# Merge gates computed first, most of them in pairs with seven products, and kept in memory until the merge

## The chip, the cores and the metric

The kernel runs on one core of one Trainium2 chip. The metric is the device time of one execution in microseconds (us); three runs of the kernel before gave 1060.51, 1060.54 and 1064.07, a median of 1060.54. A core has a matmul engine (TensorE, "PE" in the profile, with its weight loads as "PEld"), three elementwise engines (VectorE "DVE", ScalarE "ACT", GpSimd "POOL"), a queue engine (SyncE, "SP") and DMA engines between main memory and the on-chip memory (SBUF). Matmuls write into a separate small memory, PSUM, here used as eight banks of 128 x 512 numbers.

## The reference, cut to what matters

One layer over 1024 prompt tokens and 32 sample tokens (1056 columns together), width 1024. `h` is the normalised input, `w_in` one combined projection of it:

```python
z = _rmsnorm(x, norm_w) @ w_in          # qa ka va ga | qb kb vb gb | uc gc | mg (3 * 1024 wide)
# A: sliding-window attention, B: dilated attention in three groups, C: pooling  ->  oa, ob, oc
ma, mb, mc = jnp.split(mg, 3, axis=-1)
pa = (oa * jax.nn.silu(ga)) @ w_proj_a
pb = (ob * jax.nn.silu(gb)) @ w_proj_b
pc = (oc * jax.nn.silu(gc)) @ w_proj_c
m = jax.nn.sigmoid(ma) * pa + jax.nn.sigmoid(mb) * pb + jax.nn.sigmoid(mc) * pc
y = _rmsnorm(x + m @ w_out, final_norm_w)
```

The three merge gates `ma`, `mb`, `mc` are 24 blocks of 128 output channels (8 for each branch); each is a product of a 1024 x 128 weight block with the 1024 x 1056 input. The kernel also returns updated key, value and pooling states for prompt and sample.

## The kernel before, in words

Everything is computed with channels on the 128 partitions and tokens along the free axis. All dense products are in full precision made of three products of numbers in a format named `fp32r`: a number is split into a high part (ScalarE copies it into the format) and a low part (VectorE subtracts the high part from it), and hi x hi, hi x lo and lo x hi are added in PSUM.

**Projection blocks.** `w_in` is laid out as 58 blocks of 128 columns. `w_load` (L133) fetches a block of 512 KB, `w_split` (L141) splits it with one ScalarE copy and one VectorE subtraction of 128 x 1024 numbers, and `proj_chunk` (L313, matmul at L319) makes 24 matmuls (8 slices of the input width, 3 parts) for a chunk of columns. The chunks `CH` are 384, 384 and 288 columns. `project` (L334) does a whole block: it splits the next block ahead, hands out two state copies (memory to memory, issued by GpSimd, L182) and calls the evacuation of each chunk.

**Order.** The kernel is written out by hand in one order (`manual_schedule`), and each engine's instructions stand in its queue as they are written. At the start, nine input tiles are normalised and transposed while the first three blocks (K, V and the first Q of A) are made in quarters of 256, 256, 256 and 288 columns. Then follow the other projections, with the attention as side work that is pumped between matmul groups (`tick`, `pump`); then the gates of the branches, with sample attention, pooling and the merging of B's groups beside them; then the merge; then the output projection (L1480, and L1518 for the last 256 tokens) with the final norm.

**The merge (loop at L1342).** For each of 8 output blocks j and each branch: the gate block is projected (72 matmuls), each chunk is taken through tanh (`merge_gate`, L1302, sigmoid by way of tanh), then `branch` (L1289, matmul at L1295) makes the branch product of the same chunk out of the gated branch outputs `ghi`, `glo` (12 matmuls a chunk for A, 6 for B and for C), and `merge_add` (L1307) multiplies both on VectorE (L1310) and adds onto block `m_t[j]` on GpSimd (L1312). The branch outputs of C are ready before the merge; those of B and A are made during it by `gate_plan`: `load_a` fetches an attention output and its scale (DMA on SyncE, product on GpSimd, L1244), `mult_a` (L1252) multiplies it with the gate, `high` and `low` (L1265, L1271) split it. The first output block therefore takes the branches in the order C, B, A, and the others A, B, C. The eight slices of `w_out` are loaded and split in the last output block (`out_load`, `out_split`), and `m_split` (L1333) splits the merged blocks for the output projection.

## Time and profile before

| | |
|---|---|
| median of three runs | 1060.54 us |
| profiled execution, its own time | 1061.22 us |
| its span (first to last instruction) | 1059.4 us |
| TensorE busy | 1032.9 us, 97% |
| VectorE, ScalarE, GpSimd busy | 434.5, 343.2, 219.2 us |
| mean granted TensorE clock | 0.996 |
| moved by DMA | 144.43 MB |

The profile is of one execution. "Busy" is the time in which an engine had an instruction in work. TensorE's matmuls are pipelined: each is drawn longer than the distance to the next, so the price of one is taken from the distance of their starts, as the chain of waits shows it for runs of matmuls. The chain is followed back from the last instruction to what released each step. In rows of the timeline, square brackets hold the engine's idle time before an instruction and what ended it.

### The profile page before, as it was taken

The numbers are of one execution on the slowest core, as the hardware profiler recorded it, in microseconds if no ns is written. First come the engines' busy times: TensorE is split into PE (matmuls) and PEld (weight loads), VectorE is DVE, ScalarE is ACT, GpSimd is POOL, SyncE is SP. The second block draws the span as 40 slices with busy tenths as digits, with TensorE's granted clock in tenths as the row PEclk, the third lists the DMA queues.
The fourth block names the chain that finished last, engine by engine and source line by source line (L and its number), as shares of the span: only waits on it lengthen the run. The fifth ranks groups of instructions, "written<-read, shape, count | busy, mean of one in ns | idle before, by whom it ended". The sixth has DMA issues, their size and how long they took to land.

```text
span 1059.4 us, 18173 instructions
## 1 busy us (share of the span) xinstructions
PE 1032.9 (97%) x7521; PEld 992.8 (94%) x7521; DVE 434.5 (41%) x923; ACT 343.2 (32%) x842; POOL 219.2 (21%) x321
## 2 busy tenths in 40 slices
...
GB/s 253 42 213 61 61 110 116 166 59 179 81 177 98 180 136 147 107 260 309 215 288 126 230 159 78 196 104 139 79 119 157 62 175 21 89 115 101 54 71 119
DMA packets 56302, 144.43 MB, mean 136 GB/s; under 512 B 13062, under 2 KB 31812, under 8 KB 54884
## 3 DMA queue, kind: packets, MB, share of 16 engines
...
## 4 chain that ended last, share of the span: by engine, by line
PE 85%; DMA 4%; DVE 4%; ACT 2%; POOL 2%; issue 1%; ACTq 0%; POOLq 0%; SPq 0%; DVEq 0%
PE ps_pj L319 56%; PE ps_pj L1480 6%; PE ps_s L1295 4%; PE ps_t L1295 4%; PE ps_s L518 3%; PE ps_o L560 3%; DMA w_in<-w_scr 3%; PE ps_t L538 2%; PE ps_pj L1518 1%; DMA kv<-in_st_b 1%; PE ps_s L1518 1%; ACT e L525 1%; DVE sq L294 1%; PE ps_o L881 1%; POOL o_in L1166 1%
## 5 line engine op out<-in xcount | busy, mean ns | idle before, releaser
L319 PE MATMUL ps_pj<-xh,w_hi 128*128 128x384 f32 (+2 forms) x1384 | 450.9, 332 | 1.1 <-ACT xh L307 0.5
L319 PE MATMUL ps_pj<-xl,w_hi 128*128 128x384 f32 (+2 forms) x1384 | 435.6, 321 | 1.3 <-DVE xl L308 1.3
L319 PE MATMUL ps_pj<-xh,w_lo 128*128 128x384 f32 (+2 forms) x1384 | 434.7, 321 | 0.0
L319 PEld LDWEIGHTS ps_pj<-xh,w_hi 128*128 128x128 f32 x1384 | 256.5, 188 | 10.1 <-issue 6.6
L319 PEld LDWEIGHTS ps_pj<-xl,w_hi 128*128 128x128 f32 x1384 | 256.6, 188 | 1.9 <-DVE xl L308 1.5
L319 PEld LDWEIGHTS ps_pj<-xh,w_lo 128*128 128x128 f32 x1384 | 256.1, 188 | 0.0
L150 DVE TENSOR_TENSOR w_lo<-w_raw,w_hi 128x1024 fp32r<-128x1024 f32 x55 | 70.0, 1273 | 201.6 <-ACT w_hi L149 201.4
L1304 ACT ACTIVATE mth<-ps_pj 128x384 f32<-128x384 f32 (+1 forms) x72 | 33.2, 463 | 249.5 <-PE ps_pj L319 246.7
L1312 POOL TENSOR_TENSOR m<-m,mth 128x384 f32<-128x384 f32 (+1 forms) x48 | 48.0, 1018 | 286.5 <-DVE mth L1310 286.3
L410 POOL TENSOR_SCALAR k<-k 64x384 fp32r<-64x384 f32 (+1 forms) x44 | 20.8, 474 | 287.9 <-ACT k L406 211.1
L525 ACT ACTIVATE e<-e,nm_b 128x256 f32<-128x256 f32 (+1 forms) x96 | 44.2, 461 | 62.9 <-DVE nm_b L522 62.5
L149 ACT ACTIVATE w_hi<-w_raw 128x1024 fp32r<-128x1024 f32 x55 | 58.0, 1054 | 1.0 <-PE ps_pj L319 1.0
L370 DVE SCALAR_TENSOR_TENSOR q<-ps_pj,q 64x384 fp32r<-64x384 f32 (+1 forms) x62 | 31.0, 500 | 54.1 <-ACT q L369 53.8
L518 PE MATMUL ps_s<-k,q 128*128 128x256 f32 x320 | 51.2, 283 | 0.0
L518 PEld LDWEIGHTS ps_s<-k,q 128*128 128x128 f32 x320 | 45.8, 188 | 0.3 <-issue 0.2
L369 ACT ACTIVATE q<-ps_pj 64x384 fp32r<-64x384 f32 (+1 forms) x62 | 27.1, 438 | 53.6 <-DVE q L370 29.4
L538 PE MATMUL ps_t<-ident,e 128*128 128x128 f32 x276 | 43.1, 273 | 1.1 <-DVE pt L545 0.6
L182 POOL DMA_DIRECT2D out_b_s<-in_st_b x84 | 42.2, 508 | 0.0
L525 ACT ACTIVATE e<-e,nm_a 128x256 f32<-128x256 f32 (+1 forms) x64 | 31.1, 487 | 30.1 <-DVE nm_a L522 30.1
L522 DVE CUSTOM_DVE_ANT_0 e<-ps_s,bias 128x256 f32<-128x256 f32 (+1 forms) x96 | 31.8, 371 | 15.4 <-PE ps_s L518 14.9
L538 PEld LDWEIGHTS ps_t<-ident,e 128*128 128x128 f32 x276 | 33.9, 141 | 3.8 <-ACT pt L543 1.2
L560 PE MATMUL ps_o<-pt,v 128*64 128x128 f32 x552 | 35.2, 277 | 2.1 <-DVE pt L545 2.1
...
## 6 DMA issues: line engine op xcount, KB each, us to landing
...
```

Of the source, the lines that this page charges most:

```text
L149: act.activation(out=hi, in_=raw, func=AF.Copy)
L150: eng.tensor_tensor(out=lo, in0=raw, in1=hi.bitcast(F32), op=ALU.subtract)
L182: pool.dma_start(out=dst, in_=src)
L319: pe.matmul(ps[:, :cn], lhsT=parts[p][0][:, k, :], rhs=parts[p][1][:, k, c0:c0 + cn], start=(step == 0), stop=(step == 23))
L518: pe.matmul(ps[:, 256 * hd:256 * hd + 256], lhsT=q, rhs=rhs, start=(i == 0), stop=(i == 1))
L525: act.activation(out=e[:, hd, :nk], in_=e[:, hd, :nk], func=AF.Exp, scale=-1.0, bias=nm, accum_out=z)
L538: pe.transpose(tp[:, o:o + 128], e[:, hd, 128 * k:128 * k + 128], ident)
L560: pe.matmul(ps[64 * hd:64 * hd + 64, c0:c0 + 128], lhsT=v[:, tl, 64 * hd:64 * hd + 64], rhs=pt[:, o:o + 128], start=(k == 0), stop=(k == n ...
L1295: pe.matmul(pp[:, :cn], lhsT=a[:, k, :], rhs=b[k][:, c0:c0 + cn], start=(step == 0), stop=(step == last))
L1304: act.activation(out=th[:, :cn], in_=ps[:, :cn], func=AF.Tanh, scale=0.5)
L1312: pool.tensor_tensor(out=dst, in0=dst, in1=th[:, :cn], op=ALU.add)
L1480: pe.matmul(ps[o][:, :cn], lhsT=wo[k][b][:, 128 * o:128 * o + 128], rhs=a[:, k, c0:c0 + cn], start=(k == 0 and si == 0), stop=(k == 7 and ...
```

## The change

The 24 merge gates are computed first, right behind the input's normalisation, and kept in memory (`g_scr`). Gates 0 to 2 take the place that K, V and Q had in the start, gate 3 follows as an ordinary block in quarters. The other 20 blocks are taken as 10 pairs. For a pair of blocks and two of four quarters of 264 columns, the four results (two blocks x two quarters) are made from seven products of half the width (512 of 1024) instead of eight, by sums of weight halves and sums of input halves (the scheme of Winograd's variant of Strassen's product). Ten pairs times two halves of the columns are 20 iterations. In each, GpSimd makes four sums of weights for the next iteration (`pair_sums`), ScalarE and VectorE split seven weight tiles of 128 x 512 (`pair_split`; the last subtraction goes to GpSimd), TensorE makes seven products of 12 matmuls with 264 columns, VectorE combines them (`plus`), ScalarE takes the tanh and SyncE stores it (`gate_of`). The input sums are made by `combos` on VectorE and GpSimd, and split by `combo_split`.

Afterwards K, V and Q follow as ordinary projections. In the merge no gates are projected: 24 steps of branch products alone, first C (8 blocks), then B (4 blocks), A (8 blocks) and B (4 blocks); the gates are loaded from memory by SyncE (`gate_load`) into the tiles that held the input. The branch weights `w_pr` are laid out in eight tiles by branch. The output weights are prepared over steps 12 to 23, two of their subtractions on GpSimd, and all merged blocks are split before the output projection.

```diff
+    def gate_evac(g):
+        def evac(c0, cn, ps):
+            th = st.tile([128, 288], F32, tag="g", name="gate_o", bufs=8)
+            act.activation(out=th[:, :cn], in_=ps[:, :cn], func=AF.Tanh, scale=0.5)
+            sp.dma_start(out=g_scr[g][:, c0:c0 + cn], in_=th[:, :cn])
+        return evac
...
+    def combos(c):
+        a, b = st.tile([128, 8, NQ], F32, tag="s", name="x_sum", bufs=6), None
+        t1, t3 = a[:, 0:4, :], a[:, 4:8, :]
+        b = st.tile([128, 8, NQ], F32, tag="s", name="x_sum", bufs=6)
+        t2, t4 = b[:, 0:4, :], b[:, 4:8, :]
+        (h11, l11), (h12, l12) = ([t.bitcast(F32) for t in xq(2 * c, h)] for h in range(2))
+        (h21, l21), (h22, l22) = ([t.bitcast(F32) for t in xq(2 * c + 1, h)] for h in range(2))
+        add, sub = ALU.add, ALU.subtract
+        todo = [(dve, t1, h21, h22, add), (pool, t3, h11, h21, sub), (dve, t1, t1, l21, add), (pool, t3, t3, l11, add),
+                (dve, t1, t1, l22, add), (pool, t3, t3, l21, sub), (dve, t2, t1, h11, sub), (dve, t2, t2, l11, sub),
+                (dve, t4, h12, t2, sub), (dve, t4, t4, l12, add)]
+        return {"sum": (t1, t2, t3, t4), "todo": todo}
+
+    def combo_step(c, eng=None):
+        if c["todo"]:
+            e, out, x, y, op = c["todo"].pop(0)
+            (eng or e).tensor_tensor(out=out, in0=x, in1=y, op=op)
+
+    def combo_split(c, i):
+        t = st.tile([128, 8, NQ], F32R, tag="s", name=f"x_s{i}", bufs=6)
+        src = c["sum"][i - 1]
+        act.activation(out=t[:, 0:4, :], in_=src, func=AF.Copy)
+        dve.tensor_tensor(out=t[:, 4:8, :], in0=src, in1=t[:, 0:4, :].bitcast(F32), op=ALU.subtract)
+        c[i] = (t[:, 0:4, :], t[:, 4:8, :])
...
+    def pair_of(it):
+        c, i = divmod(it, 10)
+        return c, 4 + 2 * i, 5 + 2 * i
+
+    def pair_load(it):
+        if it < 20:
+            _, g1, g2 = pair_of(it)
+            raw_p[it] = w_raw(g1), w_raw(g2, True)
...
+            if (c, w) == (2, 0):
+                cmb[0] = combos(0)
+            if c >= 2:
+                combo_step(cmb[0])
+                combo_step(cmb[0])
+            if (c, w) == (3, 0):
+                pair_load(0)
...
+    def pair_sums(it):
+        r1, r2 = raw_p[it]
+        t1, t2, t3, t4 = (st.tile([128, 4, 128], F32, tag="tt", name=f"w_t{i}", bufs=6) for i in range(4))
+        for out, x, y in ((t3, r2[:, 4:8], r2[:, 0:4]), (t1, r2[:, 0:4], r1[:, 0:4]), (t2, r2[:, 4:8], t1), (t4, r1[:, 4:8], t2)):
+            pool.tensor_tensor(out=out, in0=x, in1=y, op=ALU.subtract)
+        wt[it] = {"src": {"b11": r1[:, 0:4], "b21": r1[:, 4:8], "b22": r2[:, 4:8], "t1": t1, "t2": t2, "t3": t3, "t4": t4}}
+
+    def pair_split(it, name, eng=dve):
+        if it >= 20:
+            return
+        t = w_tile({"b11": "whi", "b22": "whi", "b21": "wlo", "t4": "wlo"}.get(name, "wc"))
+        src = wt[it]["src"][name]
+        act.activation(out=t[:, 0:4, :], in_=src, func=AF.Copy)
+        eng.tensor_tensor(out=t[:, 4:8, :], in0=src, in1=t[:, 0:4, :].bitcast(F32), op=ALU.subtract)
+        wt[it][name] = t
+
+    turn7 = [0]
+
+    def product(w, x):
+        ps = bank(("pj", "s", "t", "pj", "s", "t", "pj")[turn7[0] % 7])
+        turn7[0] += 1
+        n = 0
+        for k in range(4):
+            for wo_, xo in ((0, 0), (0, 1), (4, 0)):
+                pe.matmul(ps[:, :NQ], lhsT=w[:, wo_ + k, :], rhs=x[xo][:, k, :], start=(n == 0), stop=(n == 11))
+                n += 1
+        return ps[:, :NQ]
+
+    def part():
+        return st.tile([128, NQ], F32, tag="p", name="part", bufs=6)
+
+    def plus(ps, t, out=None):
+        out = part() if out is None else out
+        dve.tensor_tensor(out=out, in0=t, in1=ps, op=ALU.add)
+        return out
+
+    def gate_of(src, g, q):
+        act.activation(out=src, in_=src, func=AF.Tanh, scale=0.5)
+        sp.dma_start(out=g_scr[g][:, NQ * q:NQ * q + NQ], in_=src)
+
+    e3 = gate_evac(3)
+    pair_sums(0)
+    pair_load(1)
+    todo = [("b11", "b21"), ("t2", "t3"), ("t1",), ()]
+    for n, (c0, cn) in enumerate(quarters):
+        for ps in proj_chunk("g3", c0, cn):
+            pass
+        e3(c0, cn, ps)
+        for name in todo[n]:
+            pair_split(0, name)
+        combo_split(cmb[0], (2, 3, 1, 4)[n])
+    pair_split(0, "t4")
+    pair_split(0, "b22")
+    for it in range(20):
+        c, g1, g2 = pair_of(it)
+        q1, q2 = 2 * c, 2 * c + 1
+        w, x = wt[it], cmb[c]
+        nxt = it + 1
+        pair_load(it + 2)
+        if it >= 18:
+            w_load(it - 18)
+        state_copy(2)
+        if nxt < 20:
+            pair_sums(nxt)
+        ps = product(w["b11"], xq(q1, 0))
+        p1 = part()
+        act.activation(out=p1, in_=ps, func=AF.Copy)
+        ps = product(w["b21"], xq(q1, 1))
+        pair_split(nxt, "b11")
+        c11 = plus(ps, p1)
+        ps = product(w["t2"], x[2])
+        u2 = plus(ps, p1, p1)
+        gate_of(c11, g1, q1)
+        pair_split(nxt, "b21")
+        if it == 9:
+            combo_split(cmb[1], 2)
+        ps = product(w["t3"], x[3])
+        u3 = plus(ps, u2)
+        pair_split(nxt, "t2")
+        if it == 9:
+            combo_split(cmb[1], 3)
+        ps = product(w["t4"], xq(q2, 1))
+        gate_of(plus(ps, u3), g1, q2)
+        pair_split(nxt, "t3")
+        ps = product(w["t1"], x[1])
+        c22 = plus(ps, u3, u3)
+        u4 = plus(ps, u2, u2)
+        gate_of(c22, g2, q2)
+        if it == 9:
+            combo_split(cmb[1], 1)
+        pair_split(nxt, "t4")
+        ps = product(w["b22"], x[4])
+        pair_split(nxt, "t1")
+        gate_of(plus(ps, u4, u4), g2, q1)
+        pair_split(nxt, "b22", pool)
+        if it == 0:
+            cmb[1] = combos(1)
+        if it < 8:
+            combo_step(cmb[1])
+            if it in (6, 7):
+                combo_step(cmb[1])
+        if it == 9:
+            combo_split(cmb[1], 4)
+        if nxt == 20:
+            w_split(0)
...
+    make_bias(0)
+    project(0, evac_k(0), 0)
+    project(1, evac_v(0), 0)
+    for i in range(4):
+        if i:
+            make_bias(i)
         if i >= 2:
             flush_attention(i - 2)
-        project(2 + i, evac_q(i), 1.6, 2)
+        project(2 + i, evac_q(i), 1.6 if i else 0, 2)
...
+    xa, xb, xc, xd = (xtp.tile([128, 4, NT], F32, tag=tag, name="x_" + tag) for tag in ("xh0", "xl0", "xh1", "xl1"))
+    temp = [xa[:, i, :] for i in range(4)] + [xb[:, i, :] for i in range(3)]
+    gate_at = [xc[:, i, :] for i in range(4)] + [xd[:, i, :] for i in range(4)] + [xb[:, 3, :]]
+    steps = [(2, j) for j in range(8)] + [(1, j) for j in range(4)] + [(0, j) for j in range(8)] + [(1, j) for j in range(4, 8)]
+    place = list(range(8)) + [8, 0, 1, 2] + [(3 + i) % 8 for i in range(8)]
+    gate_t = {}
+
+    def gate_load(i):
+        if i < 20:
+            gate_t[i] = gate_at[place[i]]
+        else:
+            gate_t[i] = mp.tile([128, NT], F32, tag=f"g{i - 20}", name="gate") if i < 22 else slot_tile(i - 22, "gate")
+        br, j = steps[i]
+        sp.dma_start(out=gate_t[i], in_=g_scr[8 * br + j])
+
+    for i in range(3):
+        gate_load(i)
...
     def load_a(i, o_slot, w_slot):
         def run():
-            t = slot_tile(o_slot, "o_in")
+            t = temp[o_slot - 1]
             sp.dma_start(out=t[:, :L], in_=o_scr[i])
-            w = slot_tile(w_slot, "w_in")
+            w = temp[w_slot - 1]
...
+    def merge_add(i, c0, cn, pp):
+        br, j = steps[i]
+        th = gate_t[i][:, c0:c0 + cn]
         dst = m_t[j][:, c0:c0 + cn]
-        out = dst if bi == 0 else th[:, :cn]
-        dve.scalar_tensor_tensor(out=out, in0=th[:, :cn], scalar=1.0, in1=pp[:, :cn], op0=ALU.add, op1=ALU.mult)
-        if bi:
-            pool.tensor_tensor(out=dst, in0=dst, in1=th[:, :cn], op=ALU.add)
+        dve.scalar_tensor_tensor(out=dst if br == 2 else th, in0=th, scalar=1.0, in1=pp[:, :cn], op0=ALU.add, op1=ALU.mult)
+        if br != 2:
+            pool.tensor_tensor(out=dst, in0=dst, in1=th, op=ALU.add)
...
+    for i, (br, j) in enumerate(steps):
...
+        if i in (0, 4, 8, 12, 14, 16, 18):
+            n = 34 + (0, 4, 8, 12, 14, 16, 18).index(i)
+            w_split(n + 1)
+            w_load(n + 3)
+        for nxt in ((3, 4, 5, 6, 7, 8) if i == 0 else (i + 8,) if 1 <= i < 9 else (i + 7,) if 10 <= i < 13 else ()):
+            gate_load(nxt)
+        if br == 1 and j == 0:
+            while gates_done[0] < 2:
+                pump()
+        if br == 0 and j == 0:
+            while gates_done[0] < 6:
+                pump()
+        if i == 1:
+            zero = mp.tile([128, 128], F32, tag="g0", name="zero")
+            pool.memset(zero, 0.0)
+            for kv in range(2):
+                sp.dma_start(out=b3_p[kv, 0:1024, :].rearrange("(p a) (b c) -> p (a b) c", a=8, c=128),
+                             in_=zero.unsqueeze(1).to_broadcast([128, 16, 128]))
...
+        if i == 22:
+            out_split(5, r[5], gh, "h2", gl, "l4", pool)
+        if i == 23:
+            out_split(6, r[6], gh, "h3", gl, "l5", pool)
+        last = i == 23
+        for c0, cn in CH[::-1] if last else CH:
+            pp = branch(i, c0, cn)
+            tick(1.0)
+            merge_add(i, c0, cn, pp)
+            if last and c0:
+                m_split(7, c0, cn)
+                if c0 == 768:
+                    out_split(7, r[7], wr, "whi", wr, "wlo")
+        if i in (14, 15, 16, 17):
+            m_split(i - 14)
+        if i in (21, 22, 23):
+            m_split(i - 17)
+    m_split(7, 0, 384)
```

## Rows read from the trace of the kernel before

**Rows 1.** Page, busy us (share of the span) and instructions.
```profile
PE 1032.9 (97%) x7521; PEld 992.8 (94%) x7521; DVE 434.5 (41%) x923; ACT 343.2 (32%) x842; POOL 219.2 (21%) x321
```

**Rows 2.** Windows: stretch, length, busy us of each engine, granted clock, DMA share, GB/s.
```profile
494.00:520.00 26.00, 23.79 (x249) 21.97 (x251) 16.14 (x26) 8.36 (x17) 16.20 (x14) 1.00 0.84 273
624.00:650.00 26.00, 26.00 (x161) 26.00 (x160) 5.43 (x8) 3.89 (x6) 4.73 (x7) 1.00 0.38 125
```

**Rows 3.** Chain of waits in order of time: start us, us, what.
```profile
42.46 2.82 PE ps_pj L319 x24
...
595.22 11.62 PE ps_pj L319 x72
...
952.13 9.54 PE ps_pj L1480 x72
```

**Rows 4.** Timeline, TensorE: first matmuls of the stages' borders.
```profile
59.86 0.42 PE L319 MATMUL ps_pj<-xh,w_hi 128*128 128x384 f32 x1
...
580.55 0.34 PE L319 MATMUL ps_pj<-xh,w_hi 128*128 128x384 f32 x1
...
951.97 0.56 PE L1480 MATMUL ps_pj<-mh,wo_hi 128*128 128x288 f32 x3
```

**Rows 5.** Groups by line and shape, GpSimd: busy us, mean ns, idle before.
```profile
L182 POOL DMA_DIRECT2D out_b_s<-in_st_b x84 | 42.2, 508 | 0.0
L1312 POOL TENSOR_TENSOR m<-m,mth 128x384 f32<-128x384 f32 x32 | 34.7, 1090 | 277.4 <-DVE mth L1310 277.1
...
L1437 POOL TENSOR_TENSOR acc<-acc,sq_o 128x512 f32<-128x512 f32 x7 | 9.1, 1298 | 32.1 <-ACT sq_o L1436 32.1
```

**Rows 6.** Groups by line and shape, ScalarE.
```profile
L1304 ACT ACTIVATE mth<-ps_pj 128x288 f32<-128x288 f32 x24 | 9.9, 411 | 38.3 <-PE ps_pj L319 38.3
...
L1335 ACT ACTIVATE mh<-m 128x512 fp32r<-128x512 f32 x8 | 4.5, 615 | 0.0
```

**Rows 7.** VectorE: a PSUM addition (groups); a split of 512 (timeline).
```profile
L1430 DVE TENSOR_TENSOR x_res<-x_res,ps_pj 128x288 f32<-128x288 f32 x6 | 2.5, 448 | 3.4 <-PE ps_pj L1480 3.4
...
963.66 0.69 DVE L1336 TENSOR_TENSOR ml<-m,mh 128x512 fp32r<-128x512 f32 x1 [1.03 <-ACT mh L1335]
```

**Rows 8.** Timeline of ScalarE and VectorE, start of the kernel.
```profile
14.61 1.05 ACT L1010 ACTIVATE w_first<-w_raw 128x1024 fp32r<-128x1024 f32 x1
...
16.76 1.44 DVE L294 SCALAR_TENSOR_TENSOR sq<-x_nat,ss,nwb 128x512 f32<-128x512 f32 x2 [0.72 <-POOL ss L286]
18.13 1.21 DVE L1011 TENSOR_TENSOR w_first<-w_raw,w_first 128x1024 fp32r<-128x1024 f32 x1
```

**Rows 9.** Timeline of VectorE and GpSimd where both have work, merge.
```profile
593.51 2.40 POOL L1244 TENSOR_TENSOR o_in<-o_in,w_in 128x1024 f32<-128x1024 f32 x1 [2.23 <-DMA w_in<-rz_scr]
...
594.46 0.55 DVE L1310 SCALAR_TENSOR_TENSOR m<-mth,ps_s 128x384 f32<-128x384 f32 x1 [0.46 <-PE ps_s L1295]
...
605.06 2.40 POOL L1244 TENSOR_TENSOR o_in<-o_in,w_in 128x1024 f32<-128x1024 f32 x1 [0.65 <-DMA w_in<-rz_scr]
605.16 3.38 DVE L150 TENSOR_TENSOR w_lo<-w_raw,w_hi 128x1024 fp32r<-128x1024 f32 x1 [3.98 <-ACT w_hi L149]
```

**Rows 10.** Windows with much DMA: start of the kernel, start of the merge.
```profile
6.00:8.00 2.00, 1.63 (x12) 1.19 (x10) 1.41 (x2) 0.13 (x1) 0.34 (x1) 1.00 1.02 418
...
588.00:592.00 4.00, 4.00 (x30) 4.00 (x29) 1.35 (x1) 2.89 (x4) 2.40 (x1) 1.00 1.06 213
```

**Rows 11.** Timeline of SyncE's queue and GpSimd, start of the merge.
```profile
580.91 0.33 SPq L1239 DMA_DIRECT2D o_in<-o_scr  x1
...
588.88 2.40 POOL L1244 TENSOR_TENSOR o_in<-o_in,w_in 128x1024 f32<-128x1024 f32 x1 [44.15 <-DMA o_in<-o_scr]
```

More of the change, by code (lines that the diff above doesn't have):

```diff
@@ L316, in proj_chunk @@
         parts = ((hi, xh), (hi, xl), (lo, xh))
-        order = [(k, p) for p in range(3) for k in range(8)] if n < 3 else [(k, p) for k in range(8) for p in range(3)]
+        first = n in ("g0", "g1", "g2")
+        order = [(k, p) for p in range(3) for k in range(8)] if first else [(k, p) for k in range(8) for p in range(3)]
         for step, (k, p) in enumerate(order):
-            pe.matmul(ps[:, :cn], lhsT=parts[p][0][:, k, :], rhs=parts[p][1][:, k, c0:c0 + cn], start=(step == 0), stop=(step == 23))
-            if step % (8 if n < 3 else 6) == (7 if n < 3 else 5):
+            pe.matmul(ps[:, :cn], lhsT=parts[p][0][:, k, :], rhs=parts[p][1][k // 4][:, k % 4, c0:c0 + cn], start=(step == 0), stop=(step == 23))
+            if step % (8 if first else 6) == (7 if first else 5):
                 yield None
@@ L1040, in build @@
     x_turn(0)
-    w_first(0)
+    w_first("g0")
     x_turn(1)
-    w_first(1)
-    x_sq(2)
-    x_scale(2)
-    w_first(2)
-    x_sq(3)
-    x_scale(3)
-    first_e = (evac_k(0), evac_v(0), evac_q(0))
+    w_first("g1")
+    norm(2)
+    w_first("g2")
+    norm(3)
+    first_e = [gate_evac(g) for g in range(3)]
     c0, cn = quarters[0]
-    runs = [proj_chunk(w, c0, cn) for w in range(3)]
+    runs = [proj_chunk(f"g{w}", c0, cn) for w in range(3)]
     for w in range(3):
@@ L1076, in build @@
                 x_turn(8)
-            if (c, w) == (2, 1):
-                w_load(4)
             if (c, w) == (3, 0):
-                w_split(3)
+                splits["g3"] = w_tile("whi"), w_tile("wlo")
+                w_first("g3")
             first_e[w](c0, cn, ps)
@@ L1088, in build @@
+    close(st_cm)
+    gc1_cm, gc1 = open_pool("gc1")
+    at_cm, at0 = open_pool("attn")
+    at[0] = at0
+    up = [gc1.tile([128, 16 + NT], F32, tag=f"c{t}", name=f"up{t}") for t in range(2)]
     for t in range(2):
```

256 lines of the change are left out of this document (104 added, 152 removed).

## The prediction

> **What bounds the kernel now.** I read the busy shares first: TensorE 97%, the three elementwise engines 21 to 41% [rows 1]. By stretches, TensorE is busy for all 26 of 26 us in the merge at full granted clock, and even where it idles a little (23.79 of 26) the clock stays 1.00 [rows 2]. The chain of waits is TensorE nearly throughout, and it gives the price of a matmul: 24 of 256 columns in 2.82 us (118 ns each), 72 of 288 in 9.54 us (132.5 ns), a whole gate block of 72 (48 of 384 columns, 24 of 288) in 11.62 us [rows 3]. TensorE's order of time gives the borders: the three quartered blocks end at 59.9, the merge runs from 580.55 to 951.97, 371.4 us, of which 24 x 11.62 = 278.9 are gates and 92.5 branch products; nothing in it is a stall [rows 4]. So the kernel is TensorE-bound, and taking columns away pays as long as the other engines keep up.
>
> **The products.** A product of the paired stage is 12 matmuls of 264 columns. Between 118 and 132.5 ns that is 121.6 ns by interpolation, 1.46 us a product, 10.2 us for the seven of an iteration, 204.3 for 20 iterations. The 20 blocks cost 20 x 11.62 = 232.4 before. TensorE's own gain is 28.1 us. Gates 0 to 2 take the place of K, V and Q of pair 0 in the start at the same matmul counts; those three then cost what the three gates did; gate 3 in quarters costs 11.7 instead of 11.62.
>
> **The paired stage: a loop through the queues.** Busy time an iteration is small: VectorE six splits at 0.69 and seven additions at 0.43, 7.2 us [rows 7]; ScalarE seven copies at 0.615, four tanh and a copy at about 0.40 (288 columns took 0.41), 6.3 us [rows 6]; GpSimd five operations of 512 elements at 1.30 and two state-copy issues at 0.51, 7.5 us [rows 5]. All stand under 10.2, so by shares the stage would be TensorE's. But the engines take their work in the written order: a weight split that was ready when ScalarE finished at 15.66 stood behind a scale that waited for GpSimd, and ran at 18.13 [rows 8]. In the new loop that order closes a ring. GpSimd starts the sums for the next iteration only behind `pair_split(nxt,"b22",pool)` of the one before, and that split waits for ScalarE's copy of b22, which is queued behind the last tanh, which waits for VectorE's last addition, which is queued behind the splits of t1 and t4, t3 and t2; and t2 is what GpSimd's sums make. Once round:
> GpSimd: two state copies 1.02, sums t3, t1, t2 3.90;
> ScalarE copies t2 0.615; VectorE splits it 0.69 and adds product 5, 0.43; tanh 0.40;
> copy t3 0.615, split 0.69, add product 6, 0.43, tanh 0.40;
> copy t4 0.615, split t4 0.69, split t1 0.69 (its copy lies beside), add product 7, 0.43, tanh 0.40;
> copy b22 0.615; GpSimd splits it 1.30.
> GpSimd 6.22, ScalarE 3.66, VectorE 4.05: 13.9 us. An instruction's hand-on costs some 0.03 to 0.08, and back-to-back operations start about as much before the end of the one ahead; I set these against each other.
>
> To it comes the conflict of VectorE and GpSimd. A VectorE split that takes 1.21 to 1.23 alone took 3.38 beside a 2.40 us GpSimd operation that it met 0.1 after its start; an operation that reads PSUM took 0.55 beside one, its usual time [rows 9]. So splits and sums exclude each other, additions do not. Placed on the loop's clock, the sum t1 falls on the split of b21 (0.4 lost) and the split of t2 on the sum t4 (0.6 lost): 14.9 us an iteration. TensorE then idles 4.7 us in each. The Trainium skill (GPSIMD Engine Reference, section 3.1 Elementwise — side-by-side cycle accounting) puts a two-input operation at about 2.6 cycles an element at 1.2 GHz; as an estimate that is 1.1 us for 512 elements, and the loop would be 14.1. The row of 1.30 decides.
>
> The first three iterations run at 10.2 on weights and banks made ahead (seven PSUM banks hold one whole iteration): 30.6, then 17 x 14.9 = 253.3. The sums of x for the second half put three GpSimd operations of 1056 elements into the loop (2.40 for 1024 [rows 9]): about 8 with VectorE's. Iteration 9 puts four copies and splits of 1056 into it: 4.5 beyond what the idle hides. Stage: 297 us. Bounds: no conflict and no extras, 17 x 13.9 + 30.6 = 267; a conflict on each of the four splits in the ring, 16.3 an iteration and 20 of extras, 328. I take 297, since conflicts are seen wherever both engines have work.
>
> Data: 1 MB of weights, 0.54 of gates out and 1 of state copies are 2.6 MB an iteration; at the 213 GB/s that mixed traffic had [rows 10] 12.2 us, under 14.9. No cost, but no room either if the loop were as fast as TensorE.
>
> **Around it.** Start: fewer evacuations, but ten sums of 1056 elements between the turns of x; +1 (-2 to +4). Hand-over to K of pair 0: `w_split(0)` stands behind the last tanh, so TensorE waits for 0.2 + 0.43 + 0.40 + 1.05 (copy) + 1.21 (split) [rows 8] = 3.3 us (2 to 5). Attention, B, pooling and sample stages keep their work, 520.7 us; the state copies run out earlier, which nothing there waits for.
>
> **The merge.** Branch products alone, 92.5 us. In the merge before, GpSimd's first product of attention output waited for its data until 588.88 after an issue at 580.91 [rows 11], covered by gate products; this cover is gone. SyncE's queue now brings nine gates (4.9 MB) ahead of that data, then 4 MB of it, 2 MB of zeros and three gates more before A can start, with 1.5 MB of weights on ScalarE's queue: 14 MB. At 418 GB/s, the best seen, 33 us; at 300, 47; at 213, 66 [rows 10]. TensorE has 12 steps of 18/72 x 11.62 = 2.9, 34.9 us, before the A steps. After the last data come 2.4 + 1.3 + 1.1 + 1.3 = 6 us of preparation. I take +18 (3 to 30), by 300 GB/s: loads are purer than in the 213 stretch. While VectorE waits in `mult_a`, the C additions queue behind it.
>
> **Tail.** GpSimd adds three pieces a step at about 1.0 [rows 5], 3.0 against TensorE's 2.9 in the last four B steps, and gets two weight splits of 2.4 among them; the last `m_split` comes that much later than the last product. The output projection needs block 7 only 8 us in. +8 (0 to 12). The rest, 107.4 us, stays.
>
> **Sum.** Paired stage 297 - 232.4 = +64.6; gate 3 +0.1; start +1; hand-over +3.3; merge +18; tail +8: +95. Against its own execution, 1061.2 + 95 = 1156.3; that execution was 0.7 above the median, so 1156. What it is told by: twenty iterations of 15 where TensorE needs 10.
>
> **Rivals.** (a) The loop does not decide, and the stage runs at TensorE's rate. For it: every engine's busy time is below 10.2, and the banks let TensorE run one iteration ahead. Against: the ring is of waits, not of load. Then the stage is 204.3: with the merge's and tail's waits 1061.2 - 28.1 + 30.4, 1063; without them 1037. The point is 11.4 us an iteration: below it, and with a merge that does not wait, the change is faster. Chance 0.13, 0.08 of it on the fast end.
> (b) TensorE's clock falls. Idle time of 4.7 us in 15, in pieces of up to 3, is more than this trace has anywhere in its middle; with 2.2 us in 26 the clock stayed 1.00 [rows 2]. At the lower of the two levels a product takes twice as long, an iteration 20.4 us. In a third of the 17: +31, 1187; in all: +94, 1250. I put it at 1200. The Trainium skill (TensorE: Matmul & The Clock Gate, section HAM oscillation — how this bites in real kernels) tells of kernels whose clock fell in each wait between groups of matmuls; no run here shows it yet. Chance 0.11.
> (c) Forecast, the ring: 0.76. Its own range, from the bounds of its terms, 1100 to 1207.
>
> From no change a measurement of this kernel tells about 0.5%, 5 us. Faster 0.08, same 0.05, slower 0.87. The range, 1095 to 1205, leaves out (a) and the upper part of (b).
>
> **What would show it.** Per iteration: 15 us between first products, TensorE idle ahead of the products of t2 and t3, VectorE idle until ScalarE's copy of t2, ScalarE until GpSimd's sum, GpSimd until the copy of b22; GpSimd sums of 1.7 and splits of 1.2 among those of 1.3 and 0.7. At the merge, VectorE waiting in `mult_a` for GpSimd, GpSimd for data. Wrong would be: iterations of 10 to 11.4 us; or a granted clock below 0.95 in the stage; or merge products without idle time.

## The result and the profile after

The changed kernel takes 1162.5 us (median of 4, 1159.7 to 1166.4) against 1060.9: ratio 1.095 [1.091, 1.100]. Forecast were 1156 and a range of 1095 to 1205. The profiled execution has a span of 1158.2 us against 1059.4, so 98.8 us are to be accounted for. (A correction to the description of the kernel before: the merge's loop stands at L1339, `branch` at L1287, `m_split` at L1332, `project` at L331.)

The page after: busy shares, then TensorE's granted clock in 40 slices.

```profile
PE 1054.4 (91%) x7785; PEld 989.1 (85%) x7785; DVE 609.7 (53%) x1157; ACT 417.4 (36%) x988; POOL 384.7 (33%) x424
...
PEclk9999999899998999999999999999999988998998
```

TensorE's share fell from 97% [rows 1] to 91%, and no other engine came near a full one: it waits, but not on a busy engine. TensorE's order of time shows the borders that answer to [rows 4]:

```profile
70.71 0.28 PE L1167 MATMUL ps_pj<-xh,w_hi 128*128 128x264 f32 x1
...
363.83 0.41 PE L1167 MATMUL ps_pj<-x_s,w_hi 128*128 128x264 f32 x2
366.49 0.69 PE L311 MATMUL ps_pj<-xh,w_hi 128*128 128x384 f32 x1 [2.25 <-ACT w_hi L142]
...
921.54 0.34 PE L1481 MATMUL ps_pj<-ghi,w_hi 128*128 128x384 f32 x1
...
1038.64 0.29 PE L1663 MATMUL ps_pj<-mxh,wo_hi 128*128 128x288 f32 x1
```

The paired products (L1167) run from 70.7 to 364.1 (the start of the last one at 363.95 and the price of one, 0.12), the projections (L311) from 366.5, the merge from 921.5, the output projection from 1038.6. Against the terms of the forecast:

| term, us | forecast | measured |
|---|---|---|
| TensorE's own gain, 20 blocks | -28.1 | -28.1 (iterations that wait for nothing take 10.2) |
| paired stage above 204.3 | +92.7 | +89.1 (293.4) |
| gate 3 and start | +1.1 | -0.8 (begins at 70.7, forecast 72.6) |
| hand-over to K | +3.3 | +2.4 |
| middle, 555.6 expected | 0 | -0.5 (555.1) |
| merge, 92.5 of products | +18 | +24.6 (117.1) |
| tail | +8 | +9.9 (1.9 and 8.0 of waits) |
| rest, 107.4 before | 0 | +2.3 |
| sum | +95 | +98.9 |

The 20 iterations, between first products, took 10.5, 10.2, 13.0, 17.5, 14.0, 17.2, 14.4, 17.0, 15.0, 15.0, 19.4, 13.7, and then eight of 14.5 to 14.6. By windows (stretch, length, busy us of PE, PEld, DVE, ACT, POOL, granted clock, DMA share, GB/s), in the order of time: two stretches of the stage's first twelve iterations, a steady one, one of the middle, one of the merge:

```profile
104.00:130.00 26.00, 20.25 (x132) 18.56 (x131) 15.28 (x22) 8.57 (x19) 15.57 (x14) 0.87 0.55 178
...
208.00:234.00 26.00, 21.20 (x131) 18.64 (x132) 18.77 (x23) 12.83 (x23) 12.50 (x12) 0.87 0.45 144
...
286.00:312.00 26.00, 21.28 (x150) 18.78 (x149) 16.45 (x23) 9.54 (x20) 15.38 (x14) 1.00 0.57 196
624.00:650.00 26.00, 26.00 (x196) 25.20 (x195) 13.14 (x43) 13.41 (x41) 8.57 (x18) 1.00 0.45 151
962.00:988.00 26.00, 15.34 (x81) 14.79 (x82) 17.50 (x23) 3.23 (x3) 17.53 (x12) 0.80 0.71 234
```

In the steady stretch the clock is 1.00 and still an iteration takes 14.5: the rival of a falling clock (b) sets no time there. It dipped to 0.87 in three and to 0.93 in one of the earlier stretches of the stage (0.96 over all of it), and to 0.80 in the merge's waits. The groups by line (busy us, mean ns, idle before and its releaser) of GpSimd and VectorE in the stage:

```profile
L1147 POOL TENSOR_TENSOR w_t<-w_raw,w_t 128x512 f32<-128x512 f32 x40 | 58.9, 1472 | 3.1
...
L1156 POOL TENSOR_TENSOR w_hi<-w_raw,w_hi 128x512 fp32r<-128x512 f32 x19 | 24.6, 1295 | 136.8 <-ACT w_hi L1155 136.8
```

```profile
L1156 DVE TENSOR_TENSOR w_c<-w_t,w_c 128x512 fp32r<-128x512 f32 x60 | 54.7, 912 | 50.5 <-ACT w_c L1155 50.5
...
L1156 DVE TENSOR_TENSOR w_lo<-w_raw,w_lo 128x512 fp32r<-128x512 f32 x20 | 38.2, 1911 | 9.3 <-ACT w_lo L1155 9.3
```

GpSimd, 33% busy over the whole run and 15.38 of 26 us in the steady stretch, waits 136.8 us for ScalarE's copy of b22, 19 times, 7.2 in the mean. Undisturbed it takes 1.30 for 512 elements, as [rows 5] had it. The Trainium skill (GPSIMD Engine Reference, section 3.1 Elementwise — side-by-side cycle accounting) gives about 2.6 cycles an element for a two-input operation, 1.1 us for 512 at 1.2 GHz as an estimate; the measurement decides. The split of b21 takes 1.91 us in the mean, where a split alone takes 0.69 [rows 7]. One steady iteration, engine by engine:

```profile
288.69 1.30 POOL L1156 TENSOR_TENSOR w_hi<-w_raw,w_hi 128x512 fp32r<-128x512 f32 x1 [6.68 <-ACT w_hi L1155]
289.93 1.01 POOL L171 DMA_DIRECT2D out_b_s<-in_st_b  x2
290.96 1.31 POOL L1147 TENSOR_TENSOR w_t<-w_raw 128x512 f32<-128x512 f32 x1
292.22 1.29 POOL L1147 TENSOR_TENSOR w_t<-w_raw,w_raw 128x512 f32<-128x512 f32 x1
293.58 2.98 POOL L1147 TENSOR_TENSOR w_t<-w_raw,w_t 128x512 f32<-128x512 f32 x2
...
295.24 0.63 ACT L1155 ACTIVATE w_c<-w_t 128x512 fp32r<-128x512 f32 x1 [3.38 <-POOL w_t L1147]
...
291.89 2.17 DVE L1156 TENSOR_TENSOR w_lo<-w_raw,w_lo 128x512 fp32r<-128x512 f32 x1 [0.50 <-ACT w_lo L1155]
295.90 1.20 DVE L1156 TENSOR_TENSOR w_c<-w_t,w_c 128x512 fp32r<-128x512 f32 x1 [1.50 <-ACT w_c L1155]
...
294.12 0.52 PE L1167 MATMUL ps_s<-xh,w_lo 128*128 128x264 f32 x2 [0.90 <-DVE w_lo L1156]
```

This is the forecast's ring: GpSimd idles 6.68 until the copy of b22, issues two state copies, sums; ScalarE idles 3.38 until the sum t2; two splits run into sums and take 2.17 and 1.20. TensorE waits for the splits at the end.

The same wait stands in the early iterations:

```profile
118.73 1.29 POOL L1156 TENSOR_TENSOR w_hi<-w_raw,w_hi 128x512 fp32r<-128x512 f32 x1 [6.67 <-ACT w_hi L1155]
133.27 1.29 POOL L1156 TENSOR_TENSOR w_hi<-w_raw,w_hi 128x512 fp32r<-128x512 f32 x1 [6.68 <-ACT w_hi L1155]
```

GpSimd comes round every 14.5 to 15.0 us, or every 17.0 where it also makes an input sum (2.92), and waits 6.67 or 6.68 in 17 of the 19 rounds, in stretches of 0.87 as of 1.00. So the ring sets the early rate too.

### The profile page after: what moved, and what is told of

Its sections match the earlier page's. It is cut to its first block, busy times and chain, and to the rows that moved or that the text cites. A ratio compares the mean times of both kernels' runs of the same rounds, so it can differ in the third digit from the quotient of the medians.

```text
span 1158.2 us, 19812 instructions
## 1 busy us (share of the span) xinstructions
PE 1054.4 (91%) x7785; PEld 989.1 (85%) x7785; DVE 609.7 (53%) x1157; ACT 417.4 (36%) x988; POOL 384.7 (33%) x424
## 3 DMA queue, kind: packets, MB, share of 16 engines
q1 hardware_dynamic: 64860, 106.21, 28.1%
## 4 chain that ended last, share of the span: by engine, by line
PE 57%; DVE 5%; POOL 5%; issue 4%; ACT 4%; DMA 3%; SPq 0%; POOLq 0%; ACTq 0%; DVEq 0%
PE ps_pj L311 33%; PE ps_pj L1663 6%; PE ps_s L510 3%; POOL w_t L1147 3%; PE ps_o L552 3%; PE ps_t L530 2%; PE ps_pj L1481 2%; DVE part L1176 1%; PE ps_t L1481 1%; PE ps_s L1481 1%; PE ps_pj L1694 1%; ACT w_c L1155 1%; DMA x_xh<-rz_scr 1%; DMA x_xl<-g_scr 1%; PE ps_s L1694 1%
## 5 line engine op out<-in xcount | busy, mean ns | idle before, releaser
L311 PE MATMUL ps_pj<-xh,w_hi 128*128 128x384 f32 (+2 forms) x912 | 298.7, 338 | 2.4 <-ACT w_hi L142 2.3
L311 PE MATMUL ps_pj<-xl,w_hi 128*128 128x384 f32 (+2 forms) x912 | 283.7, 322 | 1.0 <-DVE xl L299 1.0
L311 PE MATMUL ps_pj<-xh,w_lo 128*128 128x384 f32 (+2 forms) x912 | 283.3, 321 | 0.2 <-DVE w_lo L143 0.2
L311 PEld LDWEIGHTS ps_pj<-xh,w_hi 128*128 128x128 f32 x912 | 170.1, 191 | 10.9 <-issue 6.6
L311 PEld LDWEIGHTS ps_pj<-xl,w_hi 128*128 128x128 f32 x912 | 169.6, 190 | 1.6 <-DVE xl L299 1.3
L311 PEld LDWEIGHTS ps_pj<-xh,w_lo 128*128 128x128 f32 x912 | 169.1, 190 | 0.8 <-DVE w_lo L143 0.8
L1167 PE MATMUL ps_t<-x_s,w_c 128*128 128x264 f32 x480 | 76.4, 305 | 24.7 <-ACT w_c L1155 13.8
L1167 PEld LDWEIGHTS ps_t<-x_s,w_c 128*128 128x128 f32 x480 | 66.2, 201 | 32.0 <-ACT w_c L1155 16.9
L1167 PE MATMUL ps_s<-xh,w_lo 128*128 128x264 f32 x320 | 71.6, 301 | 17.4 <-DVE w_lo L1156 17.4
L1167 PEld LDWEIGHTS ps_s<-xh,w_lo 128*128 128x128 f32 x320 | 51.8, 188 | 25.3 <-DVE w_lo L1156 24.4
L1156 POOL TENSOR_TENSOR w_hi<-w_raw,w_hi 128x512 fp32r<-128x512 f32 x19 | 24.6, 1295 | 136.8 <-ACT w_hi L1155 136.8
L1147 POOL TENSOR_TENSOR w_t<-w_raw,w_t 128x512 f32<-128x512 f32 x40 | 58.9, 1472 | 3.1
```

Of the source, the lines that this page charges most:

```text
L311: pe.matmul(ps[:, :cn], lhsT=parts[p][0][:, k, :], rhs=parts[p][1][k // 4][:, k % 4, c0:c0 + cn], start=(step == 0), stop=(step == 23))
L1147: pool.tensor_tensor(out=out, in0=x, in1=y, op=ALU.subtract)
L1156: eng.tensor_tensor(out=t[:, 4:8, :], in0=src, in1=t[:, 0:4, :].bitcast(F32), op=ALU.subtract)
L1167: pe.matmul(ps[:, :NQ], lhsT=w[:, wo_ + k, :], rhs=x[xo][:, k, :], start=(n == 0), stop=(n == 11))
```

## Experiments: the ring

The cuts of code show the edits in part, with comments added; each ratio is to the kernel before.

**e1: the two state copies out of the ring.**

```diff
-        state_copy(2)            # in the paired loop
+        state_copy(2 * ncopy)    # in the projections instead
```

> The changed kernel without the two state copies in each iteration of the paired stage (the projections issue four instead of two, so all are still made). Theory, the ring of queues: GpSimd's two issues (2 x 0.51 us) lie in the ring, so an iteration falls from 14.5 to about 13.5 us, the stage from 293 to 276 to 282 us, the whole to about 1148 us. Rival, the stage is bound by a load (TensorE with its lowered clock, or VectorE): iterations stay at 14.5 and the time at 1160. Rival, DMA traffic slows the weight loads: iterations fall by more than 1 us, since a third of the traffic is gone.

Measured: 1155.0 us, ratio 1.090 [1.079, 1.101]; steady iterations 14.0, stage 285.7. The right direction at half the size: taking 1.0 out of the ring gave 0.5. The sums start 1.0 earlier and now meet the splits elsewhere: the first sum took 1.75 instead of 1.31, so the conflict gives half back.

```profile
285.03 1.75 POOL L1147 TENSOR_TENSOR w_t<-w_raw 128x512 f32<-128x512 f32 x1
```

**e2: the weights' sums left out** (raw halves of the weights stand in for t1 to t4).

```diff
-        t1, t2, t3, t4 = (st.tile(...) ...)    # and four GpSimd subtractions
+        t1, t2, t3, t4 = r1[:, 0:4], r2[:, 4:8], r2[:, 0:4], r1[:, 4:8]
```

> The changed kernel with the weight sums left out (the four sums are replaced by halves of the raw weights, so the gates are not the right ones). Theory, the ring: nothing that is split waits for GpSimd any more and the conflict with the sums is gone, so iterations run at 10.2 to 12 us, the stage takes about 224 us and the whole about 1093. Rival, a load: TensorE, ScalarE and VectorE have the same work as before, so iterations stay at 14 or more and the time above 1150.

Measured: 1093.2 us, ratio 1.031 [1.027, 1.036]; stage 224.1, steady iterations 11.0. The sums in the ring, with their conflicts, are 3.5 us an iteration. ScalarE, VectorE and TensorE were given the same operations as before, so it was not their load that made the 14.5.

**e3: the split of b22 on VectorE**, which opens the ring at GpSimd.

```diff
-        pair_split(nxt, "b22", pool)
+        pair_split(nxt, "b22")
```

> The changed kernel with the split of b22 wholly on VectorE: GpSimd then waits for nothing within an iteration, while VectorE gets 0.69 us more to do and the sums stay on GpSimd. Theory, the ring of waits: from iteration 12 on about 10.5 us each instead of 14.5; in the first half, where the sums of x share the port, 13 to 20 us as before; stage about 270, whole about 1139. Rival, the conflict of splits and sums alone: VectorE's splits go from six to seven, the conflict grows, iterations of 14.5 or more, whole 1162 or more.

Measured: 1142.9 us, ratio 1.078 [1.075, 1.082]; stage 270.9 as expected, but spread otherwise: the last eight iterations, expected at 10.5, go up and down from 10.6 to 15.9 (12.6 in the mean); the first twelve took 170 us, where the expected 270 had left them 186. GpSimd, no longer held by the ring, now waited 87.1 us, 12 times, for raw weights to land; why they landed late was not looked at. The sum was right by luck, its parts were not.

**e4: the same work in another order.** Each product's addition first; ScalarE's copies ahead of the tanh; all splits, and the weights' sums, on VectorE, so that the ring has no GpSimd in it.

```diff
-        pair_split(nxt, "b11")
         c11 = plus(ps, p1)
+        pair_lo(nxt, "b11")
+        pair_hi(nxt, "b21")       # ScalarE's copy of the next split
+        gate_of(c11, g1, q1)      # ... then the tanh, and so on for each product
-            pool.tensor_tensor(out=out, in0=x, in1=y, op=ALU.subtract)
+            dve.tensor_tensor(out=out, in0=x, in1=y, op=ALU.subtract)
```

> The changed kernel with the paired stage's instructions in another order: within each step VectorE's addition first, ScalarE's weight copy ahead of its tanh; weight sums, all splits and the second half's input sums on VectorE. Every engine does at least as much, VectorE some 2 us more an iteration, GpSimd only the state copies. Theory, waits and not loads: iterations of 10.2 to 10.6, about 16 where the second half's inputs are split, stage about 211 us, whole about 1080. Rival, VectorE's load binds: it has 11 operations of 0.61 and 7 of 0.35 us between starts, 9.2 us of 10.2; if its waits add 2 us, iterations of 12 and 1115.

Measured: 1124.3 us, ratio 1.061 [1.054, 1.067]. Fourteen of the 20 iterations take 10.2, TensorE's rate, with no engine but GpSimd given less to do: the ring was the cause. (With GpSimd its conflict with VectorE is gone as well; this run does not part the two.) But the stage begins at 79.1, and its first two iterations take 30.1 and 22.4. The timeline says why, GpSimd, VectorE, SyncE's queue:

```profile
43.75 4.14 POOL L171 DMA_DIRECT2D out_b_s<-in_st_b  x8
48.66 0.49 POOL L171 DMA_DIRECT2D out_b_s<-in_st_b  x1 [0.78 <-DMA out_b_s<-in_st_b]
...
83.55 0.69 DVE L1147 TENSOR_TENSOR w_t<-w_raw 128x512 f32<-128x512 f32 x1 [25.93 <-DMA w_raw<-in_w_in]
116.52 0.69 DVE L1147 TENSOR_TENSOR w_t<-w_raw 128x512 f32<-128x512 f32 x1 [21.35 <-DMA w_raw<-in_w_in]
...
61.00 29.13 SPq L1004 DMA_DIRECT2D g_scr<-gate_o  x4
92.15 0.33 SPq L1022 DMA_DIRECT2D w_raw<-in_w_in  x1
```

```profile
78.00:104.00 26.00, 13.55 (x84) 13.03 (x84) 11.56 (x15) 7.55 (x13) 7.29 (x15) 0.70 1.00 348
```

GpSimd, without work, sent the 40 state copies (0.5 MB each) off one behind the other from 43.75 on; the DMA engines are full (1.00, 348 GB/s), and VectorE waits 26 and 21 us for weights. The second pair is also issued late, from 92.15 on: SyncE stood behind its stores of gate 3 until 90.1.

**e5: e4 with the state copies held to the iterations.**

```diff
-        state_copy(2)                                  # at the top of the iteration
+        pool.tensor_copy(out=pace, in_=c11[:, 0:1])    # 0.51 us, waits for its first result
+        state_copy(2)
```

> The kernel of e4_order, in which one small GpSimd copy of a column of an iteration's first quarter of output stands in front of that iteration's two state copies, so that the idle GpSimd cannot send all 40 of them (0.5 MB each) off at once. Theory (the 43 us that e4_order lost before and in iterations 0 and 1 are the weights' loads, late behind the flood of state copies; the ring itself is gone): start of the paired stage back from 79.1 to about 71 us, iterations 0 and 1 back to 10.2 to 12, stage 245.5 to 206-215, whole about 1083. Rival (the slow first iterations come from the new order itself, whose splits of iteration 1 wait on the input sums that VectorE now makes): stage stays near 245 and the whole near 1124.

Measured: 1079.8 us, ratio 1.018 [1.015, 1.021]; the stage begins at 69.4 and takes 212.8, all iterations but 8 to 11 at 10.2. GpSimd's timeline and the same stretch as above:

```profile
76.57 0.58 POOL L1221 COPY pace<-part 128x1 f32<-128x1 f32 x1 [32.64 <-DVE part L1184]
77.10 1.29 POOL L171 DMA_DIRECT2D out_b_s<-in_st_b  x2
```

```profile
78.00:104.00 26.00, 26.00 (x216) 26.00 (x215) 25.86 (x50) 14.96 (x34) 3.25 (x7) 1.00 0.75 259
```

TensorE is busy for 26 of 26 us. The 8.5 us that stay in the stage are iterations 8 to 11 (10.4, 11.7, 13.6, 13.8), where the input's four splits come on top of a VectorE that is busy for 25.86 of 26 without them.

## Experiments: merge and tail

In the merge after, SyncE's queue, GpSimd, and TensorE's two long waits:

```profile
937.79 0.33 SPq L1414 DMA_DIRECT2D x_xh<-g_scr  x1
949.79 2.55 SPq L1539 DMA_DIRECT2D out_b_p<-zero  x2
...
957.45 0.45 SPq L1424 DMA_DIRECT2D x_xl<-o_scr  x1
...
942.43 2.34 POOL L1429 TENSOR_TENSOR x_xh<-x_xh 128x1024 f32<-128x1024 f32 x1 [57.37 <-DMA x_xh<-rz_scr]
966.52 2.34 POOL L1429 TENSOR_TENSOR x_xl<-x_xl 128x1024 f32<-128x1024 f32 x1 [16.75 <-DMA x_xl<-rz_scr]
...
946.58 0.69 PE L1481 MATMUL ps_t<-ghi,w_hi 128*128 128x384 f32 x1 [6.58 <-DVE m L1489]
970.56 0.69 PE L1481 MATMUL ps_t<-ghi,w_hi 128*128 128x384 f32 x1 [11.58 <-DVE m L1489]
```

VectorE stands in `mult_a` until GpSimd's product, that until the part's weights; behind it wait the sums that would free PSUM banks. The issue for part 2 comes only at 957.45: SyncE had waited 11.7 us, the last 4.8 of it for a tile of zeros that GpSimd fills behind its own wait. With two shorter gaps (1.4, 0.7) the waits are 20.3 of the 24.6 us. Behind the two long waits matmuls of 384 columns start 0.32 us apart, at the lower of the clock's two levels (1.2 GHz), and 0.17 apart soon after:

```profile
948.02 0.52 PE L1481 MATMUL ps_t<-glo,w_hi 128*128 128x384 f32 x1
948.34 0.52 PE L1481 MATMUL ps_t<-ghi,w_lo 128*128 128x384 f32 x1
...
951.19 0.33 PE L1481 MATMUL ps_s<-ghi,w_hi 128*128 128x384 f32 x1
951.36 0.33 PE L1481 MATMUL ps_s<-glo,w_hi 128*128 128x384 f32 x1
```

Twelve matmuls behind each wait took 3.5 and 3.8 us instead of 1.8 and 2.1: 3.4 of the other 4.3 us.

**e6: the issues moved, on the changed kernel.**

```diff
+    pump()                                         # parts 0, 1 ahead of six gate reads
-        (10, load_a(2, 5, 7)), ... (17, load_a(3, 6, 2))
+        (10, load_a(2, 5, 7, pool)), ... (17, load_a(3, 6, 2, pool))
-        if i == 1:                                 # zeros: 2 MB
+        if i == 9:                                 # filled ahead of the merge
```

> The changed kernel with three loads of the merge moved and nothing else: the tile of zeros is written before the merge and its 2 MB are sent out at step 9 instead of step 1, the loads for attention parts 0 and 1 are issued ahead of six of the gate loads, and those for parts 2 and 3 go through GpSimd's queue instead of standing in SyncE's behind gate loads that wait for merge adds. Theory (the merge's 24.6 us above its products are queueing of issues, not a lack of bandwidth): the gaps of 6.6 and 11.6 us go, the merge falls from 117 to 95-101, whole 1142-1148. Rival (the 12.6 MB of gates read back simply fill the DMA engines while TensorE waits): the gaps only move, the merge stays at 112 or more and the whole within 5 us of 1162.

Measured: 1158.8 us, ratio 1.092 [1.089, 1.095]; merge 113.1, gaps (waits of TensorE) now 5.0, 4.5 and 4.2. The theory of queued issues fell: the gaps moved. Nor do 4.0 us stand out: e1 to e5, with the merge as in the changed kernel, took 117.1 to 122.9 for it, one profile each.

**e7: the tail's splits off GpSimd, on the changed kernel.** Before it, ScalarE's last copy of the merged block waited for GpSimd's sum, and TensorE at the end of that chain:

```profile
1046.05 0.44 ACT L1516 ACTIVATE mxh<-m 128x288 fp32r<-128x288 f32 x1 [5.66 <-POOL m L1491]
...
1049.21 0.61 PE L1663 MATMUL ps_pj<-mxh,wo_hi 128*128 128x288 f32 x1 [7.98 <-DVE gate L1489]
```

```diff
-            out_split(5, r[5], gh, "h2", gl, "l4", pool)    # and 6
+            out_split(5, r[5], gh, "h2", gl, "l4")          # 7 beside it
-            pool.tensor_tensor(out=dst, in0=dst, in1=th, op=ALU.add)
+            (dve if i == 23 else pool).tensor_tensor(...)
```

> The changed kernel with the splits of output weights 5 and 6 on VectorE instead of GpSimd, that of 7 moved up beside them, and the last step's sums on VectorE. Theory (the two gaps of 1.9 and 8.0 us between merge and output projection are GpSimd's 2 splits and 3 sums, which the splits of the last quarter of the merged rows and of output weight 7 stand behind): the gaps fall to 2-3 us together, the rest is unchanged, whole 1154-1156. Rival (the gap is the load of output weight 7 that lands late): gap of about 8 us stays, whole 1160-1162.

Measured: 1165.6 us, ratio 1.097 [1.095, 1.100]; tail 7.2 (5.9 and 1.3) instead of 9.9, merge 120.1. Of the expected 7 us in the tail 2.7 came, and the whole did not fall: the merge and the middle took 3.0 and 2.5 more, no more than they vary by between these runs. VectorE's timeline there:

```profile
1045.87 1.50 DVE L1517 TENSOR_TENSOR mxl<-m,mxh 128x1056 fp32r<-128x1056 f32 x1
1047.30 3.74 DVE L1504 TENSOR_TENSOR wo_lo<-wo_raw,wo_hi 128x1024 fp32r<-128x1024 f32 x2
```

Now VectorE has the work without a pause, its splits at 1.9 instead of 1.2 beside GpSimd's sums. The load of `w_out`[7] was not the wait either.

**e8: e5, e6 and e7 in one.**

> e5_pace, e6_merge and e7_tail in one kernel: it keeps the pairs of gates and the stored gates, without the ring of queues, the state copies' flood, the queueing of the merge's loads and the GpSimd work of the end. Theory, by adding up: 1083 - 18 - 7 = 1058, so about level with the kernel before (1060.5), range 1045 to 1075. By the rival that the gates' way through memory costs bandwidth itself, 1075 or more.

Measured: 1075.8 us, ratio 1.013 [1.011, 1.015]; stage 211.3, merge 114.9 (gaps 4.4, 3.3, 7.9), tail 7.2. That is on the rival's side (1075 or more).

**e9: e8, gates read 5 steps ahead instead of 8, zeros in the last projections.**

```diff
-        for nxt in ((3, 4, 5, 6, 7, 8) if i == 0 else (i + 8,) if 1 <= i < 9 else ...
+        for nxt in ((3, 4, 5) if i == 0 else (i + 5,) if 1 <= i < 15 else ()):
```

> The kernel of e8_all with the 2 MB of zeros sent during the seventh-last projection... that is, in the last four projections before the merge, where the DMA engines were 0.36 busy in the changed kernel, and with each gate read 5 steps before its sums instead of 8, so that the reads of attention parts 2 and 3 do not share the engines with gates that are needed 20 us later. (The pace of the state copies hangs on the first product's copy instead of the first quarter of output, which should change nothing by itself.) Theory after e6_merge (the first 53 us of the merge run at the DMA engines' limit, 1.03 busy at 326-363 GB/s, so bytes and their order decide, not the queue of issues): the gaps of 4.4, 3.3 and 7.9 us shrink to 3-7 together, merge 114.9 to 98-106, whole 1075.8 to about 1065 (1058-1070). Rival (what is late is latency of single reads, from issue to landing 7-12 us whatever the traffic): gaps stay near 15, whole 1074-1077.

Measured: 1077.0 us, ratio 1.015 [1.012, 1.017]; gaps 4.9, 3.7, 4.6, merge 113.7, and the middle 562.0 instead of 554.8. A miss, on the rival's side: the merge won 1.2 us, and the middle took 7.2 more. How much of that is the zeros stays open: the middle was also 557.6 to 561.7 in e1, e6 and e7, which did not touch its end.

**e10: e8 without the reads of gates 9 to 19.**

```diff
+        if not 9 <= i < 20:
             sp.dma_start(out=gate_t[i], in_=g_scr[8 * br + j])
```

> The kernel of e8_all with the reads of 11 of the 24 gate tiles left out (those of steps 9 to 19, 5.8 MB; the sums then take whatever stands in the tile, so the merged rows are not the reference's). It measures what the gates' way back from memory costs the merge. Bandwidth theory: 5.8 MB at about 345 GB/s is 17 us of the DMA engines in the saturated 53 us, so the gaps of 3.3 and 7.9 us go and the merge falls from 114.9 to 97-102, whole about 1060. Rival (attention parts and zeros alone fill the engines, or the chain through GpSimd's products is slow by itself): merge stays above 108.

Measured: 1069.7 us, ratio 1.007 [1.005, 1.009]; merge 109.4, on the rival's side of 108: 5.8 MB less gave 5.5 us where 17 were expected. The first gap (5.9) stayed.

**e11: e8 with places for all parts** (six for gates, ten for parts), reads in the order of need and on SyncE's queue, zeros at step 15.

```diff
-    place = list(range(8)) + [8, 0, 1, 2] + [(3 + i) % 8 for i in range(8)]
+    place = [i % 6 for i in range(20)]
+    ... (1, load_a(0, 1, 2)), (4, load_a(1, 3, 4)), (9, load_a(2, 7, 8)), (15, load_a(3, 9, 10)) ...
```

> The kernel of e8_all with the merge's loads in the order in which they are needed: six places for gates instead of nine and ten for attention parts instead of seven, so that no part waits for another's place; each gate read 5 steps ahead, the parts 0 to 3 from the merge's steps 0, 1, 3 and 5 on, and the zeros at step 15. Theory after e9 and e10 (in the merge's first 50 us the four attention parts come one after the other, each load 7 to 13 us from issue to landing on engines that are full, and a 2.4 us product before the next may start; that chain is what TensorE waits for): the gaps at steps 12 and 13 go, some 4 us of waits for gates stay, merge 114.9 to 97-104, whole 1075.8 to 1060-1066. Rival (bytes alone: 16 MB are needed in the first 47 us whatever their order): merge stays at 108 or more, whole 1070 or more.

Measured: 1067.5 us (10 runs, 1061.6 to 1075.5) against 1062.2, ratio 1.006 [1.003, 1.008]; in the profiled run (1071.9, among the slower of the ten), merge 111.0 with gaps 6.7, 3.6 and 1.9. Here no part waits for another's place, and still 12 us of gaps: that chain was not the cause alone. On the whole e11 is the best version, 0.6% above the kernel before.

**e12: the changed kernel without the parts' weights** (`rz_scr`; each row read to 64 partitions).

```diff
-            for hd in range(2):    # two reads of 0.25 MB a part
+            for hd in range(0):
```

> The changed kernel without the reads of the attention parts' weights (8 reads of 0.25 MB, each row of which is spread to 64 partitions); the parts are multiplied by themselves instead, so the merged rows are not the reference's. Chain theory: the part loads' last reads are what GpSimd's product, and by it TensorE, waits for; both gaps shrink, 6.6 to about 1 us and 11.6 to about 6, merge 117 to 104-108, whole 1149-1153. Bytes theory: 2 of some 17 MB less in the first 50 us at 330 GB/s give 6 us at most, merge 111 or more.

Measured: 1154.5 us, ratio 1.087 [1.082, 1.092]; merge 108.5, gaps 4.5 and 6.0. 2 of 15 MB were worth 8.6 us, between the two theories and more than by bytes (6 us). Windows of the changed kernel with these reads in flight, then of e12 without them (last two figures: DMA share, GB/s):

```profile
937.00:942.00 5.00, 3.00 (x19) 2.68 (x17) 0.00 (x0) 0.00 (x0) 0.00 (x0) 1.00 1.03 295
942.00:946.00 4.00, 0.00 (x0) 0.00 (x0) 1.20 (x2) 0.00 (x0) 2.34 (x1) 0.67 1.05 286
```

```profile
936.00:940.00 4.00, 4.00 (x27) 4.00 (x27) 3.51 (x8) 3.12 (x3) 0.00 (x0) 1.00 1.03 422
940.00:946.00 6.00, 4.60 (x30) 4.28 (x28) 1.85 (x4) 0.00 (x0) 0.57 (x1) 1.00 1.02 406
```

With equally full engines, the plain reads (gates, attention outputs, branch weights) move at 406 to 422 GB/s, together with these reads at 286 to 295. And over the merge's first 50 us, the changed kernel and e8:

```profile
921.00:971.00 50.00, 31.84 (x187) 31.29 (x186) 24.68 (x40) 9.90 (x10) 7.20 (x4) 0.86 0.93 305
```

```profile
837.00:887.00 50.00, 38.13 (x209) 36.97 (x208) 26.55 (x45) 10.98 (x11) 11.36 (x10) 0.90 0.99 327
```

The same stretch moves 13.6 to 16.4 MB in every version of the merge, with the engines 0.83 to 1.01 busy. So I put the merge's extra mostly to the engines' time for what must be there by step 12; that is argued, not shown, since no version is without its gaps. By the byte the reads of `rz_scr` cost most (8.6 us for 2 MB, against 5.5 for 5.8 MB of gates). What the order decides (117.1 to 113.1, 114.9 to 111.0) is within the spread named at e6.

## Why the prediction was right

- **The ring** held: 14.5 against 14.9 an iteration, the idle times where they were named. e2, e3 and e4 each opened it, and only e4, with no GpSimd in it, reached the 10.2 that busy shares promised. Rival (a) fell: as written the loop took 14.5, and an iteration fell below 11.4 only without the sums (e2) or in another order (e4).
- **The conflict** was sized near and placed wrong. By 14.5 against the 13.9 of the ring alone it is some 0.6, forecast 1.0; the split of t2 lost 0.5 (1.20), forecast 0.6, but of the sums t1 kept its 1.29, and t2 with t4 took 2.98. It is no fixed addend either: with the state copies gone half of their time came back as conflict (e1).
- **The extras** came as forecast: iterations 2 to 11 are 11.2 us above 14.5 each, 12.5 were set; two first iterations ran ahead (10.5, 10.2), not three.
- **The merge** was mis-sized, 24.6 against 18. The amount was right (14 MB before part A; 15.2 moved in 50 us at 305 GB/s). Not priced were the sums of branch C behind `mult_a` (6.6 us), though the forecast names them, and the lowered clock behind the waits (3.4). Which of the loads holds the merge stays open. The 213 GB/s of [rows 10] I took for mixed traffic; e12 suggests that it is what reads of `rz_scr` do.
- **The clock** (b) went down in the stage, to 0.87 in three stretches, which the forecast had named as a sign of being wrong (below 0.95). It did not set the rate: in 104 to 182 GpSimd's wait in the ring was 6.67 or 6.68 as elsewhere, and its rounds of 17.0 were longer by an input sum. The Trainium skill (TensorE: Matmul & The Clock Gate, section HAM oscillation — how this bites in real kernels) has the clock fall in waits between groups of matmuls; here it did so around the waits of 6.6 and 11.6 us (0.67 in 942 to 946, 0.80 in 962 to 988), and in the stage in or just behind three single waits of 3.45 (ending at 111.4, 143.0 and 174.5). Short pieces do not settle it: with 4.7 of 26 us idle the clock stayed 1.00 in 286 to 312, with 4.8 it was 0.87 in 208 to 234.
- **The tail** was right in size and cause for the kernel as it stands. e7 showed that VectorE would take over as its limit.
- **The sum** came nearer than its terms, by luck: the merge (6.6), the rest (2.3) and the tail (1.9) came above the forecast, the stage (3.6), the start (1.9), the hand-over (0.9) and the middle (0.5) below.

Where the 28 us of TensorE's gain went in the best version (e11, profiled run): 7.9 in the stage, 2.1 in the hand-over, 18.5 in the merge, 7.2 in the tail. That is 35.7, more than the gain, and no version here beats the kernel before.
